# A two-layer S5, Hyena and pooling step: another opening, another order of tiles, and layer 0's output projection by halves of the tokens

## The chip, the cores and the metric

The kernel runs on one core of a Trainium2 chip. The metric is the device time of one execution in microseconds; the kernel before takes 1530.49 us (median of three runs, 1528.8 to 1534.48). The engines of the core run side by side, each through its own instructions in a fixed order: TensorE (PE, with its weight loads as PEld), VectorE (DVE), ScalarE (ACT), GpSimd (POOL) and SyncE (SP), which here issues nearly all DMAs.

## The reference

One step of a hybrid diffusion backbone of two layers. 640 tokens of 1024 numbers (512 latent ones and 128 of context) go through

```
for l in range(2):
    shift, scale, gate = split(silu(cond) @ w_mod[l] + b_mod[l])      # one row for latents, one for context
    h   = rms_norm(x, norm_g[l]) * (1 + scale) + shift
    u_a, g_a, u_b, g_b, u_c, g_c, m = split(h @ w_in[l])              # 1024 -> 7168
    y_a = s5_branch(u_a, state, ...) * silu(g_a)                      # two-way scan, 32 groups of 64 complex states
    y_b = hyena_branch(u_b, ...) * silu(g_b)                          # short conv, then long convs by FFT, order 2
    y_c = pool_branch(u_c, ...) * silu(g_c)                           # centred means over 2, 4, 8, 16 less the token
    merged = sum of sigmoid(m_i) * (y_i @ w_br_i[l])
    x = x + gate * (merged @ w_out[l])
```

and a last RMSNorm. The Hyena filters come from a small sine network over positions, `h = sin(freq*(sin(freq*(z @ w1 + b1)) @ w2 + b2)) @ w3`, times a decaying window, plus a bias; each `fft_long_conv` uses one of them. All arithmetic is float32.

## The kernel before

**Products.** Activations lie with channels on the partitions and tokens along the free side, in two halves of 320 tokens (`HT`). A float32 product is made of three matmuls: `split` (L235) rounds a tile to a high part (`wh`, a cast on ACT, L238) and takes the rest (`wl`, a subtract on DVE, L239), and `linear` (L245) adds `wh*hi`, `wh*lo` and `wl*hi` (L261 to L263). It goes through a weight tile in chunks of 128 x 512: one load `wr` of 256 KB, one cast, one subtract, and for each half of the tokens 4 x 3 matmuls of 320 columns. An input tile has two chunks. The buffers `wr`, `wh`, `wl` are three deep, and so are the PSUM tiles `mm` and those of the tag `b`.

**Opening** (`run`). The loads of the inputs, `mlp` (the filter network up to `fh`), `s5_disc` (the S5 constants), the squares of X (`square`, L577: a square on ACT and a sum over the channel tiles on DVE, L589), the chunks of the modulation (`mod_chunk`, L404), `rinv` (L610: the sum of squares by matmuls of one column, L599, then an inverse root of 13 small steps on a given engine, a diagonal `rdg` on DVE, a matmul that broadcasts it, `rbc` L635, and a copy to `rr`), `make_h` (L645) and four `filter` calls (L488: `fw`, `fwp` from `fh`, a window and bias on DVE, `fold`, and a transform `fps` L549 to L551).

**A layer** (`layer`, L1400). `u_a` (L668) makes the four input tiles of the scan, copies them to `ua`, and writes them to DRAM (`ud`), from where they come back in another layout (`ug`). Then eight S5 blocks run: `s5_gen` builds the matrices of a block (DVE and GpSimd L873 to L875, matmuls `khp`, a copy `kh`, a write `kd` to DRAM and the loads `mt` from it) and `s5_run` scans (`pz` L944, four scans on DVE, `yp` L974). Behind each block stand two or three input tiles of other branches, from the list `beside`: 12 of `conv_u` (L986: evictions to a buffer `raw`, of which there are two, a scaling on ACT and two steps on DVE, L1003 and L1005), then 4 of `gate_b` (L1030) and 4 of `ahead` (L1008), which have an eviction on ACT and little else. After the blocks come the GLU, the Hyena convolutions, the merges, and `out_proj` (L1250) with eight tiles.

**The boundary.** Between the layers the eight output tiles of layer 0, each over both halves, are followed by `rinv` on GpSimd and `make_h` for both halves; the filters of layer 1 stand between them. Layer 1's own output projection, at the end, goes through the eight tiles once for each half.

**What sets the order.** The program is written in the order above, and a scheduler at build time moves instructions against each other on each engine by estimated costs, within their dependences; on the chip every engine keeps the order that it was given. Tile pools fix how many tiles of one name may be alive.

Of the kernel before, what the change touches and what calls it, by code (L numbers as in the profile page):

```python
# [43 lines left out]
L642 = 642  # L44
PAD = 8
# [6 lines left out]
C_ID, C_ONE, C_MT, C_CM, C_DM, C_SEL, C_POSR, C_POSC, C_EL, C_ER, C_PI2, C_EPS, C_MAG, C_N = range(14)  # L52


def _cst_layout():
    sizes = [P, P, NA + NBW, CZ, H, 2, 4 * 8, 4 * 64, 15, 11, 1, 1, 1]
    offs = np.concatenate([[0], np.cumsum(sizes)])
    return [int(v) for v in offs]
# [18 lines left out]
def constants():  # L77
# [38 lines left out]
    cst[:, CO[C_MAG]] = MAGIC  # L116

# [105 lines left out]
class Body:  # L223
# [264 lines left out]
    def filter(self, l, o, hf, F, buf=None):  # L488
# [33 lines left out]
        v.tensor_tensor(out=hx[0:1, 2], in0=hx[0:1, 2], in1=br[0:1], op=ALU.add)  # L522
        v.tensor_tensor(out=hq[64:65], in0=hq[64:65], in1=br[64:65], op=ALU.add)
# [67 lines left out]

    def rsum(self, halves, tag):
# [17 lines left out]
    def rinv(self, halves, e, tag="b", root=False):  # L610
# [3 lines left out]
        ps = self.rsum(halves, tag)  # L614
# [14 lines left out]
        prs = []  # L629
        for i in range(len(halves)):  # L630
            dg = self.N.tile([P, nh, 64], F32, tag="ht", name="rdg", bufs=2)[0:64]
# [4 lines left out]
            rr = self.N.tile([P, HT], F32, tag="rr", name="rr", bufs=2)  # L636
            nc.scalar.copy(rr, pr)
            prs.append((rr, pr))
        return prs
# [5 lines left out]
    def make_h(self, l, X, half, rr):  # L645
        nc = self.nc
        sm, sg = self.smod[l]
        t0 = half * HT
        for kk in range(KD):
            t = self.N.tile([P, HT], F32, tag="ht", name="ht", bufs=2)  # L650
            for s, e, _, ci in self.segs(half):
                b = sm[:, kk, ci:ci + 1]
                hi = self.hhi[:, kk, t0 + s:t0 + e]
                lo = self.hlo[:, kk, t0 + s:t0 + e]
                if kk in (3, 6):
                    nc.gpsimd.tensor_tensor(out=t[:, s:e], in0=X[:, kk, t0 + s:t0 + e], in1=rr[:, s:e], op=ALU.mult)
                    nc.scalar.activation(t[:, s:e], t[:, s:e], AF.Identity, scale=sg[:, kk, ci:ci + 1], bias=b)
                    nc.scalar.copy(hi, t[:, s:e])
                    nc.vector.tensor_tensor(out=lo, in0=t[:, s:e], in1=hi.bitcast(F32), op=ALU.subtract)  # L659
                    continue  # L660
                nc.vector.scalar_tensor_tensor(out=t[:, s:e], in0=X[:, kk, t0 + s:t0 + e],
# [846 lines left out]
```

## Time and profile before

| | |
|---|---|
| profiled execution, us | 1534.17 |
| its span, us | 1532.4 |
| granted TensorE clock, mean over the span | 0.976 |
| median of three runs, us | 1530.49 |
| ACT, POOL busy | 44%, 34% of the span |
| cast `wh`, 128 x 512, on ACT | 0.619 us, 316 times |
| load `wr` from w_out, 256 KB, issue to landing | 3.0 us, 48 times |

The span runs from the first to the last instruction of the profiled execution; the time also holds the little that lies around it. Busy shares are averages over stages with different limits, so the stages are looked at one by one: a window of the trace gives the busy time of each engine and the clock that PE was granted there, and a list of waits tells what an engine stood idle for.

### The profile page before, as it was taken

The numbers are of one execution on the slowest core, as the hardware profiler recorded it, in microseconds if no ns is written. First come the engines' busy times: TensorE is split into PE (matmuls) and PEld (weight loads), VectorE is DVE, ScalarE is ACT, GpSimd is POOL, SyncE is SP. The second block draws the span as 40 slices with busy tenths as digits, with TensorE's granted clock in tenths as the row PEclk, the third lists the DMA queues.
The fourth block names the chain that finished last, engine by engine and source line by source line (L and its number), as shares of the span: only waits on it lengthen the run. The fifth ranks groups of instructions, "written<-read, shape, count | busy, mean of one in ns | idle before, by whom it ended". The sixth has DMA issues, their size and how long they took to land.

```text
span 1532.4 us, 28365 instructions
## 1 busy us (share of the span) xinstructions
PE 1435.3 (94%) x10812; PEld 1372.2 (90%) x10812; DVE 1125.5 (73%) x1951; ACT 672.0 (44%) x1454; POOL 524.9 (34%) x473
## 2 busy tenths in 40 slices
PE   3998899999999999999998897989999999999997
PEld 1688888999999998999997787989999999999996
DVE  8996998854777795555678879896557778866665
ACT  3574545434333342344345644544443334344443
POOL 0033433500343334553323733443003444166401
PEclk9899999999999999999998899999999999999998
DMA  9535122244322246444752342223622223322154
GB/s 313 188 112 132 57 72 70 71 146 123 99 71 77 76 134 234 157 151 139 230 159 81 110 113 68 71 71 94 172 89 81 83 70 106 115 83 83 35 178 153
DMA packets 120464, 178.74 MB, mean 117 GB/s; under 512 B 33944, under 2 KB 58152, under 8 KB 119817
## 3 DMA queue, kind: packets, MB, share of 16 engines
q1 hardware_dynamic: 115737, 170.58, 36.5%
q0 software_dynamic: 1152, 5.77, 1.1%
q8 instruction: 85, 1.39, 0.4%
q10 hardware_dynamic: 3440, 0.59, 0.2%
q14 instruction: 50, 0.41, 0.1%
HBM read 152.71 MB, written 24.18 MB: 115 GB/s over the span
## 4 chain that ended last, share of the span: by engine, by line
PE 68%; DVE 15%; DMA 6%; issue 5%; ACT 3%; SPq 2%; POOL 1%; POOLq 0%; ACTq 0%; DVEq 0%
PE mm L261 15%; PE mm L263 15%; PE mm L262 15%; PE mm L333 3%; PE mm L335 3%; PE mm L334 3%; DVE wl L239 2%; PE inva L1145 1%; SPq L914 1%; DVE i L874 1%; PE invb L1145 1%; PE yp L976 1%; PE modp L404 1%; DVE vx L1003 1%; DVE hlo L665 1%
## 5 line engine op out<-in xcount | busy, mean ns | idle before, releaser
L261 PE MATMUL mm<-hhi,wh 128*128 128x320 f32 x1408 | 446.1, 318 | 15.3 <-ACT raw L996 9.0
L263 PE MATMUL mm<-hhi,wl 128*128 128x320 f32 x1408 | 440.4, 314 | 8.5 <-DVE wl L239 6.3
L262 PE MATMUL mm<-hlo,wh 128*128 128x320 f32 x1408 | 442.4, 314 | 0.5 <-DVE hlo L659 0.4
L239 DVE TENSOR_TENSOR wl<-wr,wh 128x512 fp32r<-128x512 f32 x316 | 265.9, 843 | 114.4 <-ACT wh L238 111.5
L238 ACT CAST wh<-wr 128x512 fp32r<-128x512 f32 x316 | 195.5, 619 | 269.1 <-PE mm L262 188.9
L261 PEld LDWEIGHTS mm<-hhi,wh 128*128 128x128 f32 x1408 | 269.9, 192 | 20.8 <-ACT raw L996 10.0
L263 PEld LDWEIGHTS mm<-hhi,wl 128*128 128x128 f32 x1408 | 269.5, 192 | 9.5 <-DVE wl L239 6.8
L262 PEld LDWEIGHTS mm<-hlo,wh 128*128 128x128 f32 x1408 | 270.1, 192 | 1.7 <-DVE hlo L659 1.2
L262 PE MATMUL mm<-mlo,wh 128*128 128x320 f32 x256 | 79.6, 312 | 0.5 <-DVE mlo L242 0.4
L261 PE MATMUL mm<-mhi,wh 128*128 128x320 f32 x256 | 79.1, 312 | 0.5 <-ACT wh L238 0.4
L263 PE MATMUL mm<-mhi,wl 128*128 128x320 f32 x256 | 78.8, 309 | 0.4 <-DVE wl L239 0.4
L873 POOL TENSOR_TENSOR ow<-cw,po 128x512 f32<-128x512 f32 x32 | 41.9, 1328 | 96.6 <-PE yp L976 96.5
L875 POOL TENSOR_TENSOR i<-i,i 128x1024 f32<-128x1024 f32 x16 | 40.5, 2529 | 100.6 <-DVE i L873 71.8
L1244 DVE SCALAR_TENSOR_TENSOR mth<-mth,mm 128x320 f32<-128x320 f32 x64 | 31.1, 486 | 52.5 <-PE mm L263 52.5
L1246 POOL TENSOR_TENSOR macc<-macc,mth 128x320 f32<-128x320 f32 x32 | 35.0, 1099 | 86.4 <-DVE mth L1244 86.4
L239 DVE TENSOR_TENSOR wl<-ws,wh 128x512 fp32r<-128x512 f32 x48 | 42.7, 889 | 29.7 <-ACT wh L238 28.6
L333 PE MATMUL mm<-hhi,wh 128*128 128x320 f32 x192 | 59.9, 312 | 0.0
L335 PE MATMUL mm<-hhi,wl 128*128 128x320 f32 x192 | 59.4, 309 | 0.0
L334 PE MATMUL mm<-hlo,wh 128*128 128x320 f32 x192 | 59.4, 309 | 0.0
L238 ACT CAST wh<-ws 128x512 fp32r<-128x512 f32 x48 | 29.8, 621 | 60.2 <-PE mm L334 32.3
L1052 POOL TENSOR_TENSOR ps<-pu 128x663 f32<-128x663 f32 x8 | 12.3, 1540 | 120.4 <-ACT pu L1045 120.4
L1246 POOL TENSOR_TENSOR acc<-acc,mth 128x320 f32<-128x320 f32 x32 | 37.7, 1179 | 44.4 <-DVE mth L1244 44.3
(421 smaller groups left out, 3809.9 us busy)
## 6 DMA issues: line engine op xcount, KB each, us to landing
wr<-w_in SPq DMA_DIRECT2D x224, 256.0 KB, 2.6
wm<-w_mod SPq DMA_DIRECT2D x48, 512.0 KB, 5.4
wr<-w_out SPq DMA_DIRECT2D x48, 256.0 KB, 3.0
hd<-hs SPq DMA_DIRECT2D x32, 256.0 KB, 2.3
hsr<-hd SPq DMA_DIRECT2D x32, 256.0 KB, 2.6
mt<-kd SPq DMA_DIRECT2D x128, 32.0 KB, 1.8
wr<-w_br_a SPq DMA_DIRECT2D x16, 256.0 KB, 2.6
wr<-w_br_b SPq DMA_DIRECT2D x16, 256.0 KB, 2.7
```

Of the source, the lines that this page charges most:

```text
L238: nc.scalar.copy(hi, src)
L239: nc.vector.tensor_tensor(out=lo, in0=src, in1=hi.bitcast(F32), op=ALU.subtract)
L261: nc.tensor.matmul(ps[i], wh[:, ks], at(hi, k, sl), start=(k == 0), stop=False)
L262: nc.tensor.matmul(ps[i], wh[:, ks], at(lo, k, sl), start=False, stop=False)
L263: nc.tensor.matmul(ps[i], wl[:, ks], at(hi, k, sl), start=False, stop=(k == kt - 1))
L333: nc.tensor.matmul(out, wh[:, ks], xh, start=(k == 0), stop=False)
L334: nc.tensor.matmul(out, wh[:, ks], xl, start=False, stop=False)
L335: nc.tensor.matmul(out, wl[:, ks], xh, start=False, stop=(k == 3))
L873: eng.tensor_tensor(out=out[:, r], in0=hb(r), in1=pb(0), op=ALU.mult)
L875: e.tensor_tensor(out=out, in0=out, in1=tmp, op=ALU.add)
L1244: v.scalar_tensor_tensor(out=o[:, sl], in0=th[:, sl], scalar=1.0, in1=ps, op0=ALU.add, op1=ALU.mult)
L1246: nc.gpsimd.tensor_tensor(out=acc[:, sl], in0=acc[:, sl], in1=th[:, sl], op=ALU.add)
```

## The change

Five things are done in another way. (1) In the opening the squares are summed by PE alone, in matmuls of one column (`square_pe`), the inverse root is taken right behind them, and `make_h` goes over the tokens once, in two segments. (2) The bias of a Hyena filter, added by DVE in two operations on one partition, is added by two matmuls with one row of weights. (3) `u_a` has four buffers, two of them under the tag `raw`, and in layer 1 goes through the tiles once for each half of the tokens. (4) The list `beside` is mixed: three convolution tiles and two lighter ones to every pair of blocks, the last four channel tiles first. (5) Layer 0's output projection goes through the eight tiles once for each half, with `rinv` on DVE and `make_h` of a half behind each pass. Some memsets move from DVE to GpSimd.

```diff
@@ filter
                 nc.tensor.matmul(fp if t == 4 else fw[:, t], fh[:, t * P:t * P + P], w, start=(i == 0),
-                                 stop=(i == len(ws) - 1))
+                                 stop=(i == len(ws) - 1 and t not in (2, 4)))
+            if t in (2, 4):
+                r = slice(0, 1) if t == 2 else slice(64, 65)
+                nc.tensor.matmul(fp if t == 4 else fw[:, t], self.k(C_BR)[r], br[r], start=False, stop=True)
...
-        v.tensor_tensor(out=hx[0:1, 2], in0=hx[0:1, 2], in1=br[0:1], op=ALU.add)
-        v.tensor_tensor(out=hq[64:65], in0=hq[64:65], in1=br[64:65], op=ALU.add)
@@
+    def square_pe(self, X, kk, half, ps):
+        nc = self.nc
+        nh = HT // 64
+        sq = self.N.tile([P, HT], F32, tag="sq", name="sq", bufs=2)
+        nc.scalar.activation(sq, X[:, kk, half * HT:half * HT + HT], AF.Square)
+        for j in range(nh):
+            c = half * nh + j
+            nc.tensor.matmul(ps[:, c:c + 1], sq[:, j * 64:j * 64 + 64], self.k(C_ONE)[:, 0:1],
+                             start=(half == 0 and kk == 0 and j == 0),
+                             stop=(half == 1 and kk == KD - 1 and j == nh - 1))
@@ make_h
-    def make_h(self, l, X, half, rr):
+    def make_h(self, l, X, segs, rr):
...
-            t = self.N.tile([P, HT], F32, tag="ht", name="ht", bufs=2)
-            for s, e, _, ci in self.segs(half):
+            t = self.N.tile([P, segs[-1][1] - base], F32, tag="ht", name="ht", bufs=2)
+            for s, e, ci in segs:
...
@@ u_a
+        ua = [SP.tile([P, NT, CW], F32, name=f"ua{i}") if i < 2 else
+              SP.tile([P, NT, CW], F32, tag="raw", name="ua", bufs=2) for i in range(4)]
         for i in range(4):
-            ua = uas[i % 2]
-            nc.vector.memset(ua[:, :, 64:65], 0.0)
...
+            nc.gpsimd.memset(ua[i][:, :, 64:65], 0.0)
+        for halves in ((0,), (1,)) if l else ((0, 1),):
+            for i in range(4):
...
+                self.linear(self.I['w_in'][l, i].rearrange("p k n -> p (k n)"), KD, self.hhi, self.hlo, cb, halves)
+                if halves[-1] == 1:
+                    nc.sync.dma_start(self.ud[l].rearrange("t q c -> q t c")[i * P:i * P + P], ua[i])
@@ run, opening
+                    ssq = self.PS.tile([P, 512], F32, tag="mm", name="ssq", bufs=3)[0:64, 0:2 * (HT // 64)]
                     for kk in range(KD):
-                        self.square(X, kk, 0)
+                        self.square_pe(X, kk, 0, ssq)
...
+                    rr = self.rinv((0, 1), nc.vector, "mm", ps=ssq)
                     self.mod_turn(0, 2, self.mod_chunk(0, 2, M, "mm"), "mm")
...
-                    rr = [r for r, _ in self.rinv((0, 1), nc.vector, "mm")]
...
-                for half in range(2):
-                    self.make_h(0, X, half, rr[half])
+                self.make_h(0, X, ((0, LS, 0), (LS, T, 1)), rr)
@@ run, boundary
                             for n in range(8):
-                                self.out_proj(l, X, n, mhi, mlo, last, (0, 1))
+                                self.out_proj(l, X, n, mhi, mlo, last, (0,))
...
-                            rr = [r for r, _ in self.rinv((0, 1), nc.gpsimd, "mm")]
-                            for half in range(2):
-                                self.make_h(l + 1, X, half, rr[half])
-                            for hf in range(2):
-                                self.filter(l + 1, 1, hf, F, fb() if hf else None)
+                            rr = self.rinv((0,), nc.vector, "mm")
+                            self.make_h(l + 1, X, ((0, HT, 0),), rr)
+                            for n in range(8):
+                                self.out_proj(l, X, n, mhi, mlo, last, (1,))
+                                if n == 3:
+                                    self.filter(l + 1, 1, 0, F)
+                            rr = self.rinv((1,), nc.vector, "mm")
+                            self.make_h(l + 1, X, ((HT, LS, 0), (LS, T, 1)), rr)
+                            self.filter(l + 1, 1, 1, F, fb())
@@ layer
-            beside = [lambda i=i: self.conv_u(l, i, vx[i // 4][:, i % 4, :], SP) for i in range(12)]
-            beside += [lambda i=i: self.gate_b(l, i, S, vx[2]) for i in range(4)]
-            beside += [lambda i=i: self.ahead(l, 40 + i, AF.Tanh, 0.5, SP) for i in range(4)]
+            heavy = [lambda i=i: self.conv_u(l, i, vx[i // 4][:, i % 4, :], SP) for i in (*range(8, 12), *range(8))]
+            gates = [lambda i=i: self.gate_b(l, i, S, vx[2]) for i in range(4)]
+            ahead = [lambda i=i: self.ahead(l, 40 + i, AF.Tanh, 0.5, SP) for i in range(4)]
+            light = ahead[:2] + gates + ahead[2:]
+            beside = []
+            for i in range(4):
+                h, g = heavy[3 * i:3 * i + 3], light[2 * i:2 * i + 2]
+                beside += [h[0], g[0], h[1], h[2], g[1]]
```

PE in the opening, from the end of the filter network to the first filter: before, two stretches of modulation (`modp`) stand there; the names are those of the text above.

```order
L461 MATMUL mlpp<-mlp,w_111 128x320 x2
L404 MATMUL modp<-wm,cs 32x512 x8
L415 MATMUL modt<-cst,mp 128x2 x4
L404 MATMUL modp<-wm,cs 32x512 x4
L511 MATMUL fw_663<-w_349,fh_87 128x256 x4
L511 MATMUL fwp<-w_349,fh_87 128x256
```

The same place now:

```order
L464 MATMUL mlpp<-mlp,w_111 128x320 x2
L603 MATMUL ssq<-cst,sq 64x1 x45
L514 MATMUL fw_664<-w_406,fh_87 128x256 x3
L518 MATMUL fw_664<-br,cst 128x256
L514 MATMUL fw_664<-w_406,fh_87 128x256
L514 MATMUL fwp<-w_406,fh_87 128x256
L518 MATMUL fwp<-br,cst 128x256
```

The sums of squares have come to this place, the modulation has left it for later, and each filter has two matmuls more.

ScalarE in the first S5 blocks of layer 0: before, one convolution tile (`raw`) follows another.

```order
L996 COPY raw<-mm 128x320
L238 CAST wh<-wr 128x512
L996 COPY raw<-mm 128x192
L996 COPY raw<-mm 128x128
L1001 ACTIVATE vx_1051<-raw,par_143 128x642
L238 CAST wh<-wr 128x512
L996 COPY raw<-mm 128x320
```

The same place now, where `gst` is the result of an `ahead` tile:

```order
L1017 COPY raw<-mm 128x192
L1017 COPY raw<-mm 128x128
L1022 ACTIVATE vx_1054<-raw,par_143 128x642
L241 CAST wh<-wr 128x512
L1034 ACTIVATE gst<-mm 128x320
L241 CAST wh<-wr 128x512
L1034 ACTIVATE gst<-mm 128x320
```

A lighter tile stands behind the first convolution tile.

PE at the end of the boundary: before, the broadcasts `rbc` of both halves stand among the transforms of layer 1's filters.

```order
L550 MATMUL fps<-flo,fr 128x256
L551 MATMUL fps<-fhi,fr 128x256
L635 MATMUL rbc<-rdg,cst 128x320 x2
L550 MATMUL fps<-flo,fr 128x256
L551 MATMUL fps<-fhi,fr 128x256
```

The same place now, behind the tiles of the second half:

```order
L614 MATMUL ssq<-cst,acc 64x1 x5
L554 MATMUL fps<-flo,fr 128x256
L555 MATMUL fps<-fhi,fr 128x256
L614 MATMUL ssq<-cst,sq 64x1 x5
L652 MATMUL rbc<-rdg,cst 128x320
L264 MATMUL mm<-hhi,wh 128x320
L265 MATMUL mm<-hlo,wh 128x320
L266 MATMUL mm<-hhi,wl 128x320
```

The broadcast of the second half stands between the last sums of squares and the first matmuls of the scan input of the first half, with nothing else there.

## Rows read from the trace of the kernel before

**Rows 1.** Page, part 1: engine, busy us, share of the span, instructions.
```profile
PE 1435.3 (94%) x10812; PEld 1372.2 (90%) x10812; DVE 1125.5 (73%) x1951; ACT 672.0 (44%) x1454; POOL 524.9 (34%) x473
```

**Rows 2.** Windows, layer 0 blocks: stretch, length, busy PE, PEld, DVE, ACT, POOL; granted clock, DMA.
```profile
145.00:195.00 50.00, 46.16 (x460) 44.35 (x461) 46.92 (x63) 24.61 (x65) 20.09 (x11) 0.97 0.22 67
195.00:244.00 49.00, 45.15 (x408) 43.51 (x408) 43.01 (x71) 27.52 (x70) 16.41 (x12) 0.93 0.28 75
244.00:295.00 51.00, 45.36 (x388) 44.49 (x385) 43.86 (x54) 23.59 (x62) 23.22 (x16) 0.93 0.24 71
295.00:341.00 46.00, 46.00 (x455) 45.26 (x454) 30.76 (x38) 15.51 (x38) 10.94 (x11) 1.00 0.38 111
```

**Rows 3.** The same for the blocks of layer 1.
```profile
895.00:945.00 50.00, 43.93 (x456) 42.07 (x454) 47.60 (x66) 24.81 (x66) 21.59 (x12) 1.00 0.21 61
945.00:994.00 49.00, 44.65 (x406) 43.64 (x408) 41.42 (x67) 27.51 (x70) 16.00 (x11) 0.93 0.27 76
994.00:1044.00 50.00, 44.53 (x393) 43.66 (x388) 43.57 (x55) 23.38 (x62) 23.59 (x16) 0.97 0.24 72
1044.00:1089.00 45.00, 45.00 (x448) 44.27 (x447) 30.15 (x38) 15.40 (x37) 10.25 (x11) 1.00 0.39 111
```

**Rows 4.** Windows of DVE line L1003, one a convolution tile: stretch, length, busy, count.
```profile
244.00:295.00 51.00, 4.45 (x3) 0.93 0.24 71
295.00:341.00 46.00, 0.00 (x0) 1.00 0.38 111
```

**Rows 5.** PE's waits in 145 to 345: waiting line, releaser, us in total, times, longest.
```profile
PE yp L974 <- DMA mt<-kd: 8.0, 4, 3.6
PE mm L261 <- ACT raw L996: 5.1, 2, 3.1
```

**Rows 6.** PE's waits in 895 to 1095.
```profile
PE yp L974 <- DMA mt<-kd: 11.5, 5, 3.7
PE mm L261 <- ACT raw L996: 3.9, 2, 2.6
```

**Rows 7.** Windows, the boundary between the layers, and the last output projection.
```profile
800.00:845.00 45.00, 38.31 (x246) 33.71 (x247) 37.09 (x78) 26.54 (x59) 13.30 (x21) 0.89 0.27 94
845.00:880.00 35.00, 27.36 (x157) 26.58 (x157) 29.45 (x35) 22.02 (x53) 27.71 (x19) 0.85 0.38 104
738.70:880.00 141.30, 126.98 (x832) 121.24 (x832) 107.25 (x187) 72.05 (x157) 56.51 (x60) 0.93 0.47 144
1487.00:1515.50 28.50, 28.39 (x197) 26.95 (x196) 19.29 (x43) 14.30 (x28) 2.55 (x3) 1.00 0.65 206
```

**Rows 8.** PE's longest wait in 738 to 895.
```profile
PE mm L263 <- DVE wl L239: 5.0, 1, 5.0
```

**Rows 9.** Windows, the opening: both parts up to the first DRAM round trip.
```profile
0.00:36.50 36.50, 10.39 (x32) 4.00 (x32) 30.00 (x111) 13.20 (x28) 1.47 (x6) 0.95 0.94 310
36.50:130.00 93.50, 86.16 (x588) 70.29 (x589) 84.04 (x178) 55.94 (x127) 24.86 (x20) 0.93 0.46 145
```

**Rows 10.** One of PE's waits in 0 to 130.
```profile
PE mm L263 <- DVE ua L672: 2.3, 1, 2.3
```

**Rows 11.** PE timeline 0 to 60: start, us of the run, engine, line, tiles, count.
```profile
26.02 4.45 PE L404 MATMUL modp<-wm,cs 128*32 128x512 f32 x16
...
39.61 1.99 PE L511 MATMUL fw<-w,fh 64*128 64x256 f32 x8
...
58.31 0.74 PE L599 MATMUL ssq<-cst,acc 128*64 128x1 f32 x10
```

**Rows 12.** DVE line L589: ns min/median/max, first and last start, shapes.
```profile
L589 DVE TENSOR_TENSOR acc<-acc,sq x12: 480/483/485, 19.5 to 40.3; 128x320 f32<-128x320 f32 x12
```

**Rows 13.** DVE lines by shape in 845 to 880: count, busy us, mean ns, idle.
```profile
L239 DVE TENSOR_TENSOR wl<-wr,wh 128x512 fp32r<-128x512 f32 x7 | 10.4, 1492 | 5.5 <-ACT wh L238 5.5
```

**Rows 14.** The same in 1458.5 to 1515.5.
```profile
L239 DVE TENSOR_TENSOR wl<-wr,wh 128x512 fp32r<-128x512 f32 x29 | 19.8, 689 | 9.7 <-ACT wh L238 9.7
```

**Rows 15.** POOL timeline, first step of the inverse root at the boundary.
```profile
809.23 0.20 POOL L626 TENSOR_SCALAR ry<-rx 64x10 int32<-64x10 int32 x1 [12.51 <-ACT rx L625]
```

More of the change, by code (lines that the diff above doesn't have):

```diff
@@ L44 @@
 L642 = 642
+RAW = NT * CW
 PAD = 8
@@ L116, in constants @@
     cst[:, CO[C_MAG]] = MAGIC
+    for r in (0, 64):
+        cst[r, CO[C_BR] + r] = 1.0 / (1.0 + f32(0.05))
     fmax = 15
@@ L608, in newton, with rinv @@
         e.tensor_tensor(out=y, in0=y, in1=t, op=ALU.mult)
-    def rinv(self, halves, e, tag="b", root=False):
+    def rinv(self, halves, e, tag="b", root=False, ps=None):
         nc = self.nc
@@ L613, in rinv @@
         n = nh * len(halves)
-        ps = self.rsum(halves, tag)
+        if ps is None:
+            ps = self.rsum(halves, tag)
         x = self.N.tile([64, n], F32, tag="rx", name="rx", bufs=2)
@@ L652, in make_h @@
                 b = sm[:, kk, ci:ci + 1]
-                hi = self.hhi[:, kk, t0 + s:t0 + e]
-                lo = self.hlo[:, kk, t0 + s:t0 + e]
+                hi = self.hhi[:, kk, s:e]
+                lo = self.hlo[:, kk, s:e]
+                tv, rv = t[:, s - base:e - base], rr[:, s - base:e - base]
                 if kk in (3, 6):
[L656 to L659, printed above, removed]
+                    nc.gpsimd.tensor_tensor(out=tv, in0=X[:, kk, s:e], in1=rv, op=ALU.mult)
+                    nc.scalar.activation(tv, tv, AF.Identity, scale=sg[:, kk, ci:ci + 1], bias=b)
+                    nc.scalar.copy(hi, tv)
+                    nc.vector.tensor_tensor(out=lo, in0=tv, in1=hi.bitcast(F32), op=ALU.subtract)
@@ L660, in make_h @@
                     continue
-                nc.vector.scalar_tensor_tensor(out=t[:, s:e], in0=X[:, kk, t0 + s:t0 + e],
-                                               scalar=sg[:, kk, ci:ci + 1], in1=rr[:, s:e], op0=ALU.mult,
-                                               op1=ALU.mult)
-                nc.scalar.activation(hi, t[:, s:e], AF.Identity, bias=b)
-                nc.vector.scalar_tensor_tensor(out=lo, in0=t[:, s:e], scalar=b,
-                                               in1=hi.bitcast(F32), op0=ALU.add, op1=ALU.subtract)
@@ L668, in u_a @@
-    def u_a(self, l, S, uas):
+                nc.vector.scalar_tensor_tensor(out=tv, in0=X[:, kk, s:e], scalar=sg[:, kk, ci:ci + 1], in1=rv,
+                                               op0=ALU.mult, op1=ALU.mult)
+                nc.scalar.activation(hi, tv, AF.Identity, bias=b)
+                nc.vector.scalar_tensor_tensor(out=lo, in0=tv, scalar=b, in1=hi.bitcast(F32),
+                                               op0=ALU.add, op1=ALU.subtract)
+    def u_a(self, l, SP):
         nc = self.nc
+        ua = [SP.tile([P, NT, CW], F32, name=f"ua{i}") if i < 2 else
+              SP.tile([P, NT, CW], F32, tag="raw", name="ua", bufs=2) for i in range(4)]
@@ L987, in conv_u @@
         nc = self.nc
-        raw = U.tile([P, L642 + 2], F32, tag="raw", name="raw", bufs=2)
+        raw = U.tile([P, RAW], F32, tag="raw", name="raw", bufs=2)
         nc.vector.memset(raw[:, 0:1], 0.0)
@@ L1009, in ahead @@
         nc = self.nc
-        st = U.tile([P, L642 + 2], F32, tag="raw", name="gst", bufs=2)[:, 0:T]
+        st = U.tile([P, RAW], F32, tag="raw", name="gst", bufs=2)[:, 0:T]
         def cb(half, ps):
```

36 lines of the change are left out of this document (17 added, 19 removed).

## The prediction, made before the changed kernel had run

> **What bounds the kernel now.** I read the busy shares first. TensorE (PE) is busy for 94% of the span and VectorE (DVE) for 73% [rows 1], so time can only come from PE's idle stretches, from stretches in which PE was granted less than its full clock, and from PE instructions that go away. The second view is a table of windows cut at the kernel's stages, read by two columns: PE's busy time against the window's length, and the granted clock. In each layer's eight S5 blocks the first three pairs of blocks leave PE 3.8 to 6.1 us short, mostly at 0.93 to 0.97 of its clock, while the last pair has no idle time and the full clock [rows 2, 3]. The same rows show what differs: DVE is busy for 85 to 95% of the first three windows and for 67% of the last. The 12 convolution tiles (evicted by ScalarE into a buffer called raw, then one ScalarE and two long DVE steps each) all end in the first three windows, three of them in the third and none in the last [rows 4], which has light tiles alone. Third, the waits of PE in these stretches: 8.0 and 11.5 us for the loads of mt (a block's kernel matrix, which goes out to DRAM and comes back), 5.1 and 3.9 us for the two raw buffers [rows 5, 6].
>
> The boundary between the layers (second half of the output projection, inverse root, make_h, the next layer's scan input u_a) takes 141.3 us, of which PE is busy 126.98 at 0.93 of the clock; the idle 14.3 us lie after 800 us, about half in front of the scan input (800 to 845) and half within it (845 to 880) [rows 7]. The longest single wait there is 5.0 us for a DVE subtract [rows 8]. In the opening PE does 10.39 us of work in the first 36.5 us and is nearly full, 86.16 of 93.5 us at 0.93, from there to the first DRAM round trip [rows 9].
>
> Everything is summed against the profiled execution, 1534.2 us (span 1532.4 and 1.8 around it); it lies 3.7 us above the median of 1530.5.
>
> **The opening.** Removed from DVE: 12 additions of 0.483 us, 5.8 us [rows 12], of which ten start before 36.5 us, where DVE is the engine that the filter network goes through (30.0 us busy) [rows 9]. Some small S5 steps are pulled ahead in their place, so I let the first filter matmul come 3 us sooner than 39.61 [rows 11]. The squares' sums become 80 matmuls of one column instead of 20; ten took 0.74 us, so 80 cost 5.9 us, all in PE's idle 26 us at the front [rows 9, 11]. But the modulation leaves that place: 24 of its matmuls stood ahead of the first filter, at 4.45/16 = 0.28 us each 6.7 us, and now come behind it [rows 11]. Behind the first filter PE therefore gets +6.7, -1.5 (20 old sum matmuls), and +2.0 for the bias: eight matmuls with one row of weights, which no row shows; the nearest, 64 rows deep, is 1.99/8 = 0.25 us [rows 11] (ends 0.1 and 0.4 us each). That makes +7.2 us against 7.3 us of idle there [rows 9]. The wait for a reused ua buffer, 2.3 us, goes with four buffers [rows 10]. The eight one-row bias additions that leave DVE I count at nothing, since PE is the fuller engine there, and the memsets that go to GpSimd as well, which is busy for 1.47 of the first 36.5 us [rows 9]. Of the idle I let half be filled: 7.2 - 3 - 3.7 = 0.5. I take 0; ends -5 (all the idle filled, the early start kept, half of the 6 us that 7% of the clock is worth) and +8 (nothing hides).
>
> **The S5 blocks.** The new order gives three convolution tiles and two light tiles to every pair of blocks. DVE's load is then the mean of the four windows, 164.6/196 = 84% in layer 0 and 162.7/194 = 84% in layer 1 [rows 2, 3]. What can be won at most is the idle time, 13.3 and 15.9 us, and the clock, 7.7 and 4.5 us (busy time by one minus the clock, window by window): 41 us, and that is one end. The other end has a row too: the third window already has three convolution tiles and light ones beside them [rows 4], a load of 86 or 87%, and it stalls as the others do, 51 us against 46 and 50 against 45 for the last [rows 2, 3]. If every pair became like the third, layer 0 would take 4 x 51 = 204 instead of 196 and layer 1 200 instead of 194: +14. But the third pair inherits what the second left on DVE, and it has no part in the waits for raw, which come where convolution tiles follow each other. So the value that I take is nearer to that row than to the last: the 9.0 us of waits for raw go [rows 5, 6], since two convolution tiles now follow each other directly only once in a pair of blocks, and 2 us of clock with them; the 19.5 us of waits for mt stay, since their chain (an eviction by ScalarE, one DVE step, a DRAM write and read) has the same PE work beside it as before and DVE is no emptier than in the third window. -11; ends +14 and -41.
>
> **The boundary.** Done half by half, the first half's inverse root and make_h lie under eight half tiles of PE work, and the second half's make_h under the scan input of the first half. The pattern itself has a row: the last output projection, half by half already, keeps PE busy 28.39 of 28.5 us [rows 7]. So the 6.7 us of idle in 800 to 845 go, and with them the clock lost there, 11% of 38.3 = 4.2 us. Of the 7.6 us of idle and 4.1 us of clock in 845 to 880 most stays: it comes from GpSimd and DVE preparing the S5 matrices together, which is not moved; I let 3 us go. Against it stand the bias matmuls, +2.0, and one new wait: the broadcast of the second half's inverse root stands in PE's queue directly ahead of the scan input, which does not need it but is queued behind it. From the last sums to it are a ScalarE step, 13 small steps (0.20 us each on GpSimd [rows 15], now on DVE: 2.6 us) and the diagonal. With what lies between the steps I take 4.5 us; if other DVE work stands between, 8.
>
> Each half needs its own weights: 16 more chunk loads, casts and subtracts in the projection and 8 in the scan input. The loads are 24 x 256 KB beside a DMA share of 0.47, and the casts go to ScalarE, which is busy for 72 of the 141 us [rows 7]; both are hidden. The subtract took 0.69 us where GpSimd was nearly idle [rows 7, 14] and 1.49 where GpSimd was busy for 27.7 of 35 us [rows 7, 13]. So 16 x 0.69 + 8 x 1.49 = 23 us on DVE, which has 107.25 of 141.3 us there: 130 us, below the 95% that DVE reaches in its fullest window [rows 3]. I hide them. Sum: +2.0 + 4.5 - 6.7 - 4.2 - 3 = -7.4, taken as -7; ends +7 (nothing recovered) and -17 (all idle and all lost clock recovered).
>
> Stretches with waits are the ones below the full clock here: 0.89 and 0.85 against 1.00 [rows 7]. The Trainium skill (TensorE: Matmul & The Clock Gate, "Why this matters for your kernels") asks for no idle gaps between bursts of matmuls. By it the new 4.5 us wait would be followed by a stretch at the lower clock; if that cost as much as the 4.2 us lost in 800 to 845, the boundary would be -3 and the time 1519.
>
> **The sum.** 0 - 11 - 7 = -18: 1534.2 - 18 = 1516; from the median it would be 1512.5. I say 1515.
>
> **The rivals.**
> 1. Every pair of blocks becomes like the third. The mechanism: DVE is at 84 to 87% everywhere, the one DVE step in the chain to mt stands behind convolution steps in all eight blocks, and the last pair loses its light load. For it: the third window [rows 2 to 4]. Against it: the mean over the layer holds two windows that are fuller. The blocks give +14, the rest -7: 1541. The break-even of the whole change is at blocks +7, that is 0.9 a pair, pairs of 49.9 us in layer 0 and 49.4 in layer 1; it is slower by more than noise from pairs of 50.8 and 50.3.
> 2. Much more is won. For it: the last pair at 67% has no idle at all, so the stalls may end at a load between 67 and 85%, and the clock comes back with the waits. Blocks -28, boundary -10, opening -3: 1493. Against it: the third window, and 7 us more PE work behind the first filter.
> 3. The change does not do what it says at the boundary: the broadcast ahead of the scan input keeps the old wait in a new place, 8 us and the clock behind it, so the boundary gives +4 instead of -7, with the blocks' -11: 1527. For it: nothing stands between the two on PE; against it: the step is one of 320 tokens, behind short work.
> 4. DVE becomes the bound at the boundary: the second half's make_h, the S5 preparation and the chunk subtracts in one queue, with three chunk buffers between DVE and PE; one such wait is there already, 5.0 us [rows 8]. At a mean of 2.1 us for a subtract, 24 are 50 us; (107.25 + 50)/0.95 = 166 us instead of 141, +25; with the blocks' -11 the time is 1548. Break-even with -11 is where DVE has 152 x 0.95 = 145 us, a mean subtract of 1.6 us. Against it: the 16 in the projection meet little GpSimd work, and a mean of 0.96 is what I expect.
>
> **Chances and range.** The forecast, within 1504 to 1526, has 0.45; rival 1 (1530 to 1550) 0.10; rival 2 (1483 to 1504) 0.24; rival 3 (1518 to 1533) 0.14; rival 4 (1533 to 1560) 0.07. A change of 0.5%, 7.7 us, is about what a measurement of this kernel can tell from none; within it is 1522.8 to 1538.1. Faster: most of the forecast (0.40), all of rival 2 and a third of rival 3 (0.05): 0.69. Slower: 0.06 of rival 1 and 0.04 of rival 4: 0.10. The rest, 0.21, is no change. The forecast's own range is 1504 to 1526; 1492 to 1536 leaves out two fifths of rival 2, half of rival 1 and most of rival 4, 0.20 together.
>
> **What would show it.** Right: the four pairs of blocks look like each other, 48 to 49 us each, with no wait for raw over 1 us and PE's waits for mt still 15 to 22 us in both layers together; the output projection of layer 0 in two stretches of about 30 us with PE full; one wait of 4 to 5 us of PE on the broadcast, then the scan input; the subtract's mean below 1.5 us there; the first filter matmul at about 36 us and the end of the first scan input within 4 us of 130. Wrong: pairs of 51 us (rival 1) or of 46 (rival 2); a wait on the broadcast above 7 us (rival 3); several waits of PE for wl at the boundary (rival 4); the first scan input later than 134 us, for which the sum has no room.

## The result, and the profile after

The changed kernel takes 1549.44 us (median of four runs, 1547.79 to 1552.48) against 1531.53 us of the kernel before: ratio 1.0117, 95% interval 1.0089 to 1.0144. It is slower by 1.2%, and the time lies 13 us above the wider of the prediction's ranges (1492 to 1536).

PE is as busy as before by share, and does more in a longer span (part 1 of the page, to [rows 1]):

```profile
PE 1463.0 (94%) x10964; PEld 1392.9 (90%) x10964; DVE 1117.6 (72%) x1943; ACT 684.7 (44%) x1469; POOL 525.3 (34%) x474
```

From the traces, the moments at which the stages begin or end, in us from the span's start (first or last instruction on the tile named):

| | before | after | difference |
|---|---|---|---|
| first scan matmul `pz`, layer 0 | 145.0 | 152.0 | +7.0 |
| first step of the GLU (`ghi`), layer 0 | 349.2 | 356.7 | +7.5 |
| first matmul of the output projection | 734.7 | 739.7 | +5.0 |
| last `X` of layer 0 | 801.5 | 838.2 | +36.7 |
| end of make_h for layer 1 | 844.2 | 858.5 | +14.3 |
| first `pz`, layer 1 | 894.8 | 912.7 | +17.9 |
| first `ghi`, layer 1 | 1098.5 | 1114.7 | +16.2 |
| last `X` of layer 1 | 1520.1 | 1536.9 | +16.8 |

So there are two losses: 7 us in the opening and 13 us at the boundary (173.0 us from the first projection matmul to the first scan matmul, 160.1 before). The blocks with the mixed order of tiles changed by +0.5 and -1.7 us, the stretches behind them by -2.5 and +0.6, far from the -11 forecast. These moments are of one execution each: layer 0's blocks take 206.0 and 200.9 us in two traces of one kernel (mixed_only and mixed_again, below), so a difference of a few us in one stage says little by itself.

**The opening.** Windows up to the end of the first scan input (columns as in the windows above), against [rows 9]:

```profile
0.00:36.50 36.50, 21.70 (x162) 18.96 (x163) 28.10 (x108) 14.18 (x31) 3.12 (x14) 1.00 0.88 289
36.50:54.00 17.50, 17.50 (x52) 11.77 (x51) 15.71 (x45) 10.20 (x23) 0.00 (x0) 1.00 0.36 88
54.00:137.00 83.00, 77.55 (x481) 60.48 (x481) 60.14 (x87) 42.44 (x92) 26.37 (x19) 0.98 0.48 154
```

The clock column reads 1.00 in the second row, and PE is busy all the time. The timeline of PE shows what this hides (start, us, operation, tiles, count):

```profile
16.49 7.63 PE L603 MATMUL ssq<-cst,sq 128*64 128x1 f32 x70 [3.76 <-ACT sq L600]
...
26.47 6.56 PE L603 MATMUL ssq<-cst,sq 128*64 128x1 f32 x60
...
37.25 2.92 PE L514 MATMUL fw<-w,fh 64*128 64x256 f32 x6
40.10 1.22 PE L518 MATMUL fw<-br,cst 1*128 1x256 f32 x2
...
53.89 1.92 PE L514 MATMUL fw<-w,fh 64*128 64x256 f32 x6
55.74 0.69 PE L518 MATMUL fw<-br,cst 1*128 1x256 f32 x2
...
62.63 1.92 PE L407 MATMUL modp<-wm,cs 128*32 128x512 f32 x16
64.48 1.56 PE L514 MATMUL fw<-w,fh 64*128 64x256 f32 x6
```

Six records of the same filter matmul take 2.92 us at 37.25 and 1.56 us at 64.48: until 53.9 us PE ran at half speed, the lower of its two levels. The 160 records of one-column matmuls ahead of it ran at that level too (60 records in 6.56 us, 1.1 us for ten, where ten took 0.74 us [rows 11]) and did not lift it. In the kernel before, the modulation stood there. It began at the lower level as well (16 records in 4.45 us [rows 11], 1.92 us later in that trace), and the first filter behind it ran at full speed at once, 8 records in 1.99 us [rows 11]. 16.6 us at half speed are 8 us of work. The kernel before has such a stretch too, but a shorter one: from 60.2 to 66.6 us, behind 30 records of one-column matmuls, and there the granted clock reads 0.50 (60 to 66 us). The rows also show that an fp32 matmul leaves two records: 80 one-column matmuls are 160 records and took 7.6 + 6.6 + 3.5 = 17.7 us, and a bias matmul is two, 1.2 us at half and 0.69 at full speed.

From 36.5 us to the first scan matmul, before and after:

```profile
36.50:145.00 108.50, 97.84 (x668) 81.71 (x668) 91.36 (x191) 61.98 (x140) 28.28 (x22) 0.94 0.50 148
36.50:152.00 115.50, 110.05 (x674) 87.03 (x673) 83.05 (x149) 59.04 (x128) 28.77 (x20) 0.99 0.51 147
```

PE stands idle for 5.4 us instead of 10.7, so half of the idle time was filled, as forecast. But its work grew by 12.2 us, where 7.2 were forecast. By lines of the kernel: the bias matmuls 7.1 us, the filter matmuls 5.6 more (at half speed), the modulation 2.3 more, the sums of squares 2.5 less.

**The boundary.** The whole stretch, before and then after, and three stretches of after:

```profile
734.70:894.80 160.10, 144.14 (x991) 137.91 (x990) 119.92 (x208) 79.56 (x173) 62.54 (x63) 0.94 0.49 147
```

```profile
739.70:912.70 173.00, 150.01 (x1014) 140.48 (x1013) 138.19 (x240) 94.61 (x200) 62.26 (x58) 0.93 0.58 175
845.00:860.00 15.00, 13.84 (x77) 13.28 (x77) 13.03 (x34) 11.97 (x30) 4.22 (x12) 0.83 0.27 86
860.00:880.00 20.00, 15.78 (x96) 13.76 (x94) 15.25 (x13) 14.03 (x31) 14.57 (x12) 1.00 0.57 170
880.00:898.00 18.00, 8.45 (x43) 8.45 (x44) 18.00 (x17) 8.18 (x23) 13.87 (x8) 0.72 0.41 92
```

DVE has 18 us more to do (138.2 against 119.9). The subtracts alone are 21.8 us more, near the 23 that the prediction had for them (before, then after):

```profile
L239 DVE TENSOR_TENSOR wl<-wr,wh 128x512 fp32r<-128x512 f32 x28 | 25.7, 922 | 12.2 <-ACT wh L238 12.1
L242 DVE TENSOR_TENSOR wl<-wr,wh 128x512 fp32r<-128x512 f32 x53 | 47.5, 902 | 15.9 <-ACT wh L241 15.6
```

Over the stretch DVE is 80% busy. But from 880 to 898 us it is busy for 18.00 of 18 us and PE for 8.45. PE's waits in 743 to 900, to [rows 8]:

```profile
PE mm L266 <- DVE wl L242: 13.8, 6, 9.6
PE mm L264 <- ACT wh L241: 3.5, 2, 3.2
PE rbc L652 <- DVE rdg L649: 3.5, 1, 3.5
```

The wait on the broadcast is 3.5 us, 4.5 forecast. The waits for `wl` are 13.8 us, where the kernel before had 5.0 in one wait [rows 8]; 9.6 us of them are one wait. DVE's timeline ahead of its end at 889.55 us:

```profile
877.80 1.54 DVE L894 TENSOR_TENSOR i<-bb,pi 128x512 f32<-128x512 f32 x1
879.26 1.54 DVE L895 TENSOR_TENSOR i<-bb,pi 128x512 f32<-128x512 f32 x1
880.73 1.54 DVE L894 TENSOR_TENSOR i<-bb,pi 128x512 f32<-128x512 f32 x1
882.19 1.53 DVE L895 TENSOR_TENSOR i<-bb,pi 128x512 f32<-128x512 f32 x1
883.65 3.10 DVE L940 TENSOR_TENSOR tt<-ph 128x352 f32<-128x352 f32 x2
886.67 5.75 DVE L242 TENSOR_TENSOR wl<-wr,wh 128x512 fp32r<-128x512 f32 x3
```

The subtracts of three chunks start at 886.67, behind six steps of the S5 preparation (`i`, `tt`) that take 1.5 us each, and take 1.9 us each themselves (0.69 where GpSimd is nearly idle [rows 14]). The scan input's second half, which PE has in its queue, stands still for that long.

This order is not new. In mixed_only, a run below that has the boundary of before, the same steps stand ahead of a subtract that PE stands still for, 5.6 us; the list of waits puts it down to DVE's memset of `raw`, which ends right behind that subtract (872.90 us; a row of its waits and one of DVE's timeline):

```profile
PE mm L266 <- DVE raw L1011: 5.6, 1, 5.6
870.06 2.84 DVE L242 TENSOR_TENSOR wl<-wr,wh 128x512 fp32r<-128x512 f32 x1
```

So what the halves changed is the length of the wait, 9.6 us instead of 5.0 to 5.6. By halves a chunk has 12 matmuls behind it and not 24, with three chunk buffers as before, so PE can run out of chunks sooner while DVE is at the preparation. That fits, but no run tests it by itself.

**The S5 blocks.** Windows of layer 0 after, to [rows 2], and PE's waits in the blocks of layer 0, then of layer 1, to [rows 5, 6]:

```profile
152.00:203.00 51.00, 47.10 (x472) 45.81 (x472) 45.12 (x64) 24.18 (x64) 21.38 (x12) 0.97 0.30 89
203.00:252.00 49.00, 47.14 (x439) 45.93 (x438) 36.91 (x57) 26.35 (x66) 19.97 (x14) 0.93 0.24 70
252.00:302.00 50.00, 45.03 (x428) 43.46 (x428) 43.60 (x59) 25.06 (x64) 22.08 (x16) 1.00 0.24 71
302.00:352.00 50.00, 48.20 (x417) 47.58 (x412) 32.00 (x50) 17.38 (x42) 5.50 (x7) 0.97 0.38 109
```

```profile
PE yp L995 <- DMA mt<-kd: 5.5, 3, 2.4
PE yp L997 <- DVE w L989: 4.2, 3, 1.6
PE mm L264 <- ACT raw L1017: 1.8, 2, 1.1
```

```profile
PE mm L264 <- ACT raw L1017: 7.5, 2, 6.6
PE yp L997 <- DVE w L989: 3.7, 5, 1.1
PE yp L995 <- DMA mt<-kd: 3.2, 2, 2.1
```

The stalls are spread, not gone: no window is free of idle time any more, waits for `mt` fell from 19.5 to 8.7 us, waits for `w` (the scan's result on DVE) grew from 0.7 to 7.9 us, and `raw` is at 9.3 us, 9.0 before. DVE's load did not become even: it is 88, 75, 87 and 64% of the four windows, though two or three convolution tiles end in each. In the last window their first step takes 0.88 us on DVE and GpSimd is busy for 5.5 us; in the second it takes 1.57 us and GpSimd is busy for 20.0. So the last pair of blocks was not light on DVE through its light tiles alone.

### The profile page after: what moved, and what is told of

It is laid out like the page before. It is cut to its first block, busy times and chain, and to the rows that moved or that the text cites. A ratio compares the mean times of both kernels' runs of the same rounds, so it can differ in the third digit from the quotient of the medians.

```text
span 1549.7 us, 28772 instructions
## 1 busy us (share of the span) xinstructions
PE 1463.0 (94%) x10964; PEld 1392.9 (90%) x10964; DVE 1117.6 (72%) x1943; ACT 684.7 (44%) x1469; POOL 525.3 (34%) x474
## 4 chain that ended last, share of the span: by engine, by line
PE 70%; DVE 13%; DMA 6%; issue 5%; ACT 3%; POOL 2%; SPq 2%; POOLq 0%; DVEq 0%; ACTq 0%
PE mm L264 14%; PE mm L266 14%; PE mm L265 14%; PE mm L336 3%; PE mm L338 3%; PE mm L337 3%; DVE wl L242 2%; PE modp L407 2%; PE inva L1166 1%; PE yp L997 1%; PE invb L1166 1%; PE fw L514 1%; DVE kk L983 1%; DVE i L895 1%; DVE kk L982 1%
## 5 line engine op out<-in xcount | busy, mean ns | idle before, releaser
L242 DVE TENSOR_TENSOR wl<-wr,wh 128x512 fp32r<-128x512 f32 x340 | 286.9, 845 | 108.8 <-ACT wh L241 105.5
L241 ACT CAST wh<-wr 128x512 fp32r<-128x512 f32 x340 | 210.1, 618 | 277.3 <-PE mm L265 200.3
L896 POOL TENSOR_TENSOR i<-i,i 128x1024 f32<-128x1024 f32 x16 | 44.1, 2758 | 88.6 <-DVE i L894 67.3
L338 PE MATMUL mm<-hhi,wl 128*128 128x320 f32 x192 | 59.4, 309 | 0.0
L337 PE MATMUL mm<-hlo,wh 128*128 128x320 f32 x192 | 59.4, 309 | 0.0
L241 ACT CAST wh<-ws 128x512 fp32r<-128x512 f32 x48 | 29.8, 621 | 60.2 <-PE mm L337 32.3
L264 PEld LDWEIGHTS mm<-mhi,wh 128*128 128x128 f32 x256 | 49.7, 195 | 7.2 <-ACT wh L241 5.6
```

Source lines behind the costliest of these rows:

```text
L241: nc.scalar.copy(hi, src)
L242: nc.vector.tensor_tensor(out=lo, in0=src, in1=hi.bitcast(F32), op=ALU.subtract)
L264: nc.tensor.matmul(ps[i], wh[:, ks], at(hi, k, sl), start=(k == 0), stop=False)
L337: nc.tensor.matmul(out, wh[:, ks], xl, start=False, stop=False)
L338: nc.tensor.matmul(out, wl[:, ks], xh, start=False, stop=(k == 3))
L896: e.tensor_tensor(out=out, in0=out, in1=tmp, op=ALU.add)
```

## The experiments

The times are medians; the ratios are to runs of the kernel before on the same chip. First the parts of the change one by one.

**dve_bias.**

```diff
-                nc.tensor.matmul(fp if t == 4 else fw[:, t], self.k(C_BR)[r], br[r], start=False, stop=True)
...
+        v.tensor_tensor(out=hx[0:1, 2], in0=hx[0:1, 2], in1=br[0:1], op=ALU.add)
+        v.tensor_tensor(out=hq[64:65], in0=hq[64:65], in1=br[64:65], op=ALU.add)
```

> The changed kernel with the Hyena bias added by DVE again (16 matmuls with one row of weights out). Theory: PE is the bound in both places where filters stand, so they cost their full time: 8 x 0.63 us at the boundary, about 6.6 us in the opening (three of them at 1.15 us): 1549 - 11 = 1538, within 1534 to 1543. Rival, the bias matmuls lie beside other work: 1547 to 1551.

1551.63 us, ratio 1.0126 (1.0106 to 1.0145): nothing won. My theory on the bias matmuls fell. Without them PE stands idle for 13.5 us from 36.5 us to the first scan matmul instead of 5.4, partly for the first filter's results (rows of PE, with the wait in brackets):

```profile
48.77 0.58 PE L552 MATMUL fps<-fhp,frp 128*128 128x256 f32 x1 [2.78 <-ACT fhp L241]
50.94 0.58 PE L552 MATMUL fps<-fhi,fr 128*128 128x256 f32 x1 [1.58 <-ACT fhi L241]
```

and the filter's records stay at half speed until 59.4 us instead of 53.9. The first scan matmul comes at 153.6 us, against 152.0.

**mod_front.**

```diff
-                    rr = self.rinv((0, 1), nc.vector, "mm", ps=ssq)
                     self.mod_turn(0, 2, self.mod_chunk(0, 2, M, "mm"), "mm")
...
                     self.mod_turn(0, 0, self.mod_chunk(0, 0, M, "mm"), "mm")
+                    rr = self.rinv((0, 1), nc.vector, "mm", ps=ssq)
```

> The changed kernel with the inverse root of the opening called behind the third modulation chunk, as before; the squares are still summed by 80 matmuls of one column, but the modulation stands among them and among the first filters again. Theory: the first filters run at half speed from 37 to 54 us because PE had only one-column matmuls to do before; with the 512-column matmuls of the modulation there they run at full speed, 4 to 8 us are won: 1541 to 1545. Rival, the one-column matmuls in front are themselves the loss (18 us of PE): 1548 to 1551.

1562.76 us, ratio 1.0198 (1.0173 to 1.0222): the opposite of what I expected, the first scan matmul at 162.2 us. The first filter did run at full speed, and the next one no longer; the window shows the clock that was granted from 54 to 97 us:

```profile
47.15 1.56 PE L514 MATMUL fw<-w,fh 64*128 64x256 f32 x6
...
59.15 2.93 PE L514 MATMUL fw<-w,fh 64*128 64x256 f32 x6
```

```profile
54.00:97.00 43.00, 43.00 (x157) 28.50 (x154) 26.04 (x55) 14.73 (x30) 3.87 (x4) 0.60 0.22 74
```

PE was busy all the time and at 0.60 of the clock for 43 us, 17 us of work lost. So the modulation in front did not secure the speed. It fell at about 50.5 us, right behind 20 records of one-column matmuls; the fall at 60.2 us in the kernel before has 30 of them ahead of it.

**old_opening** (with the inverse root as in mod_front and the bias as in dve_bias).

```diff
-                        self.square_pe(X, kk, 0, ssq)
+                        self.square(X, kk, 0)
...
-                self.make_h(0, X, ((0, LS, 0), (LS, T, 1)), rr)
+                self.make_h(0, X, ((0, HT, 0),), rr)
+                self.make_h(0, X, ((HT, LS, 0), (LS, T, 1)), rr[:, HT:])
```

> The changed kernel with the opening of before (squares summed on DVE, inverse root late, make_h by halves) and the bias on DVE everywhere; boundary by halves and mixed tiles kept. Theory: the opening's 7 us and the 5 us of bias matmuls at the boundary go: 1549 - 12 = 1537, 1534 to 1540, first scan matmul at about 145. Rival, the loss is all in the boundary's DVE work: 1545 or more.

1542.67 us, ratio 1.0065 (1.0044 to 1.0086): the first scan matmul is at 145.4 us, so the opening's 7 us are back. They are not the clock alone: from 36.5 us to the first scan matmul PE was granted 0.89 of it here, less than before (0.94), and had stretches at half speed too (0.50 from 48 to 54 us).

```profile
36.50:145.40 108.90, 99.95 (x668) 84.36 (x668) 86.64 (x192) 63.12 (x140) 27.43 (x22) 0.89 0.51 152
```

The boundary is as long as in the changed kernel (172.9 us), so the bias matmuls cost nothing there.

**old_boundary.**

```diff
-        for halves in ((0,), (1,)) if l else ((0, 1),):
+        for halves in ((0, 1),):
...
-                                self.out_proj(l, X, n, mhi, mlo, last, (0,))
+                                self.out_proj(l, X, n, mhi, mlo, last, (0, 1))
...
+                            rr = self.rinv((0, 1), nc.gpsimd, "mm")
```

> The changed kernel with the boundary of before (out_proj over both halves, inverse root on GpSimd, make_h for both halves behind it, u_a of layer 1 over both halves at once); opening, bias matmuls and mixed tiles as changed. Theory: the boundary from the first output-projection matmul to the first scan matmul, 173 us in the changed kernel and 160 before, goes back to 160 plus 5 for the bias matmuls: 1549 - 8 = 1541, 1538 to 1545. Rival, the halves hide make_h as meant and the loss is elsewhere: 1549 or more.

1536.19 us, ratio 1.0031 (1.0016 to 1.0046): 13 us back; the boundary takes 161.7 us.

**mixed_only** and, in more rounds, **mixed_again** (old_opening and old_boundary together: the mixed order, four `ua` buffers and memsets on GpSimd remain).

> The kernel before with the mixed order of input tiles alone (and the four ua buffers and the memsets on GpSimd; opening, bias on DVE and boundary as before). Theory: the stages of the changed kernel put the mixed order at -0.5 and +0.5 us in the two layers' S5 blocks and -2.4 us in each layer's stretch behind them: 1526, 1523 to 1530. Rival 1 of the prediction (every pair like the third): 1540 or more.

> The mixed order alone once more, in more rounds: is it faster than the kernel before? From the first time: ratio 0.9986, between 0.997 and 1.000.

1528.25 us, ratio 0.9986 (0.9974 to 0.9999), and 1528.66, ratio 0.9975 (0.9959 to 0.9991). It is faster than the kernel before by 0.1 to 0.3%; rival 1 of the prediction is out.

Then the boundary.

**filters_behind.**

```diff
+                            wd = F.tile([P, 256], F32, tag="w3", name="w3", bufs=1)
+                            nc.scalar.copy(wd[:, 0:1], X[:, KD - 1, T - 1:T])
                             rr = self.rinv((1,), nc.vector, "mm")
```

> The changed kernel with the last two filters of layer 1 held back by a dependence until the last X of the second half is there (one copy of 128 numbers), so that the second half pass is projection alone and the filters' matmuls stand behind the broadcast, among the scan input. Theory now: the boundary is a chain, last X, inverse root, make_h, S5 preparation (which waits for the space of X) and scan input; in the changed kernel all filters were done before the last X, which came 31.7 us later after the start of the projection than before (98.5 against 66.8), and left PE nothing to do beside the chain. The last X comes about 15 us sooner, the first scan matmul of layer 1 10 to 15 us sooner: 1535 to 1540. Rival, DVE's subtracts behind the S5 preparation are the loss: DVE has the same work, 1547 to 1552.

1550.49 us, ratio 1.013 (1.0114 to 1.0147): that theory fell. The last X did come 13 us sooner, at 825.2, but make_h ended at 860.6 (858.5 in the changed kernel): DVE now had the filters' windows and folds in between and was full,

```profile
845.00:860.00 15.00, 15.00 (x111) 14.50 (x109) 14.73 (x32) 11.09 (x27) 4.13 (x6) 1.00 0.36 121
```

as the third busy time of the window, DVE's, shows (14.73 of 15 us).

**whole_ua.**

```diff
-        for halves in ((0,), (1,)) if l else ((0, 1),):
+        for halves in ((0, 1),):
```

> The changed kernel with the scan input of layer 1 done over both halves at once (8 chunk loads, casts and subtracts fewer), the output projection by halves kept. Theory (chain from the last X): the chain is the same and the scan input must now wait for the second half's make_h, but needs half of the subtracts: within 4 us of the changed kernel, 1546 to 1554. Rival, the 8 added subtracts of 1.1 us beside the S5 preparation are the loss: 1538 to 1542.

1541.64 us, ratio 1.0064 (1.0043 to 1.0085): 8 us back, as the rival had it. From the end of make_h to the first scan matmul there are 48.7 us, 54.2 in the changed kernel. What is left to old_boundary, 5 us, is the projection by halves beside a whole scan input.

**ua_halves** (against old_boundary).

```diff
-        for halves in ((0, 1),):
+        for halves in ((0,), (1,)) if l else ((0, 1),):
```

> The run old_boundary (1536: output projection over both halves, inverse root on GpSimd) with the scan input of layer 1 by halves again. Theory: the halved scan input costs 5 to 7 us wherever the projection stands: 1541 to 1544. Rival, the halves let the scan input start under the second half's make_h and the loss came from the projection by halves: 1530 to 1536.

1550.16 us, ratio 1.0123 (1.0091 to 1.0154): 14 us more than old_boundary, again with one wait of 9.6 us for `wl`. It is also as slow as the changed kernel, which has the projection by halves as well: the two costs do not add, and beside a halved scan input the halved projection costs nothing that these times show. In the two traces the difference is 10 us: 6.7 us lie before the first scan matmul, about 4 in the S5 blocks behind it; why those are longer I can't say.

**split_twice.**

```diff
             self.split(wh, wl, wr)
+            if twice:
+                self.split(wh, wl, wr)
```

> The mixed order alone (run mixed_only, 1528), with the cast and the subtract of each of the 8 weight chunks of layer 1's scan input done twice into the same buffer; loads and matmuls are unchanged. That is the DVE and ScalarE work that the halved scan input adds, and nothing else of it. Theory now: beside the S5 preparation DVE and GpSimd are the bound, so the 8 subtracts lengthen the stretch from the end of make_h to the first scan matmul of layer 1 from 49.4 to 54 or 55 us, as in every run with the halved scan input: 1533 to 1536. Rival, it is the order of the halves (the second half's chunks behind the first, more loads), not the split work: 1526 to 1530.

1537.94 us, ratio 1.0037 (1.0024 to 1.0051), against 0.9986 for mixed_only beside the same kernel: 8 to 10 us for 8 casts and 8 subtracts, with neither loads nor matmuls more. The boundary grew from 159.3 to 166.6 us. PE waits for `wl` 9.5 us in all, 5.6 in mixed_only (above), but the longest wait is as long as there, 5.5 us, and not 9.6:

```profile
PE mm L268 <- DVE wl L242: 9.5, 2, 5.5
```

So the added DVE and ScalarE work costs time there, in other waits than the halves do. A chunk's second cast also has to follow its first subtract here, which reads what that cast writes, a chain that the halves do not have; the run does not tell the two apart.

**quiet.**

```diff
-        kr(e, ow, o1, self.cw, self.po, 1)
+        if l == 1 and b < 2:
+            e.memset(ow, 0.0)
+        else:
+            kr(e, ow, o1, self.cw, self.po, 1)
```

> The changed kernel with GpSimd's share of the S5 preparation left out in the first two blocks of layer 1 (the output matrices ow are set to zero there in place of seven GpSimd steps each, so layer 1's scan output of these blocks is not computed). DVE's order from make_h to the first scan matmul is the same: six S5 steps stand ahead of the subtract that PE waited 9.6 us for. Theory, each is slow because GpSimd works beside it: from 880 us on they take 0.7 instead of 1.5 us, the wait falls to 5 us or less, the first scan matmul of layer 1 comes 4 to 9 us sooner, 1540 to 1545. Rival, the order alone is the loss: the wait stays at 8 us or more, 1546 to 1550.

1544.37 us, ratio 1.008 (1.0057 to 1.0103), 5 us less. From the end of make_h to the first scan matmul of layer 1 there are 49.8 us, 54.2 in the changed kernel; another 4.8 us in this trace were won ahead of the output projection, where the edit changes nothing. DVE's order is the same, its steps are not (to compare with the timeline above):

```profile
877.25 0.68 DVE L895 TENSOR_TENSOR i<-bb,pi 128x512 f32<-128x512 f32 x1
877.86 0.68 DVE L894 TENSOR_TENSOR i<-bb,pi 128x512 f32<-128x512 f32 x1
878.46 0.68 DVE L895 TENSOR_TENSOR i<-bb,pi 128x512 f32<-128x512 f32 x1
879.06 3.12 DVE L943 TENSOR_TENSOR tt<-ph 128x352 f32<-128x352 f32 x2
882.10 1.88 DVE L242 TENSOR_TENSOR wl<-wr,wh 128x512 fp32r<-128x512 f32 x3
```

```profile
PE mm L266 <- DVE wl L242: 8.5, 7, 4.9
```

Three of the four `i` steps take 0.68 us instead of 1.54 and the subtracts 0.63 instead of 1.9, and the longest wait for `wl` is 4.9 instead of 9.6 us. So about half of that wait is this work of GpSimd beside DVE. What remains is the order, the subtracts behind the preparation, with what GpSimd still does there. The kernel before has that order, and a wait of 5.0 us, with all of GpSimd's work.

Last, the opening once more. **old_squares** (the inverse root stays early).

```diff
-                        self.square_pe(X, kk, 0, ssq)
+                        self.square(X, kk, 0)
...
-                self.make_h(0, X, ((0, LS, 0), (LS, T, 1)), rr)
+                self.make_h(0, X, ((0, HT, 0),), rr)
+                self.make_h(0, X, ((HT, LS, 0), (LS, T, 1)), rr[:, HT:])
```

> The changed kernel with the squares of the opening summed on DVE again (12 additions, 20 one-column matmuls instead of 80) and make_h by halves; the inverse root is called early as changed, so the modulation stays behind the first filters. Theory: the opening's 7 us come from the modulation and the bias matmuls behind the first filters, while PE has run at half speed until then; the 60 further one-column matmuls lie in idle time and cost nothing: first scan matmul at 150 to 154, 1547 to 1551. Rival, the one-column matmuls are the loss: first scan matmul at 145 to 148, 1541 to 1545.

1562.28 us, ratio 1.0224 (1.0173 to 1.0276), the first scan matmul at 159.6 us: neither expectation. With the modulation gone to later and no one-column matmuls in its place, PE is idle for 9 us ahead of the first filter and at half speed until 56 us. It falls to half speed again at 59.3 us (granted 0.77 from 60 to 66), with filter and bias matmuls ahead of it and no one-column ones, so the falls in these traces have no one cause that I can name. Taking either half of the new opening back makes it worse; taking both back helps. Which part of it the 7 us are, no run shows.

## Why the prediction was wrong

- **The opening, "I take 0"**: it was +7, and the terms that failed are the work behind the first filter, +7.2 forecast and +12.2 measured, and "all in PE's idle 26 us at the front" with no price for the speed behind it. The sum read the timeline's counts as matmuls; they are records, two for each of these matmuls, and those of the modulation in front were at half speed. So the 80 sums cost 17.7 us and not 5.9; the eight bias matmuls 7.1 us and not 2.0 (an end of the range had 3.2); the modulation 2.3 more and not 6.7. The filter matmuls, which had no term at all, cost 5.6 us more, since the first 16.6 us behind the one-column matmuls ran at half speed. Half of the idle time was filled, as forecast, and the first filter came 2.4 us sooner, 3 forecast. Why the whole is 7 us later stays open: without the bias matmuls PE waits instead (dve_bias), a full-speed first filter did not help (mod_front), and old_opening won the 7 us back with a mean clock of 0.89. Shown is only that it is the new opening, of which neither half can go back alone.
- **The S5 blocks, -11**: -1 by the table, -3 us in the whole time with all that mixed_again wins. The step that failed is the load: "DVE's load is then the mean of the four windows" came out as 88, 75, 87 and 64% in layer 0. The 9 us of waits for `raw` did not go; those for `mt`, which I had let stand, fell by 11 us, and new ones for the scan's DVE steps took 7 us in their place. The bound that I had from the third window (+14) was too pessimistic.
- **The boundary, -7**: +13. The new wait on the broadcast was sized about right (3.5 for 4.5 us), and so was DVE's added work (21.8 for 23 us). The step that failed is "I hide them", of the chunk preparation that halving doubles: 8 chunks more in the scan input cost 8 us beside the halved projection (whole_ua) and 14 without it (ua_halves), the projection's halves 5 us or nothing. I compared DVE's load with the length of the whole stretch, 130 of 141 us; but PE waits for particular subtracts, which stand behind the S5 preparation, where DVE is busy for 18.00 of 18 us from 880 us on, and the wait that was 5.0 us became 9.6. GpSimd's work beside DVE is about half of that (quiet); the rest is argued from the order, not tested.
- **Rival 4** named the place, the queue and a time of 1548, and had a chance of 0.07. Its time came near by luck, +25 at the boundary with -11 in the blocks, where +13, -1 and the opening's +7 were measured. Its price was wrong as well: it asked for a mean subtract above 1.6 us, and the mean was 0.90 over the boundary and 1.09 from 843 us on. Not the mean tells but which instructions stand ahead of a subtract that PE is waiting for.
- **The lower clock behind a wait** was at the boundary as the second reckoning had it: the windows behind the wait on the broadcast and around the 9.6 us wait were granted 0.83 and 0.72. The Trainium skill (TensorE: Matmul & The Clock Gate, "Why this matters for your kernels") asks for no idle gaps between bursts of matmuls. Here the trace agrees: 0.50 was granted from 845 to 850 us, right behind the first of these waits, and 1.00 from 850 to 860.

## What to carry to other kernels

Cost work that is added to an engine in the stretch where it lands, against what is already queued there, not against the stage's mean load: DVE at 76% over 141 us did not hide 8 more subtracts in the 40 us in which GpSimd works beside it. Halving a product over its tokens doubles the weights' preparation and leaves each prepared chunk half of the matmuls; here it cost up to 14 us. Before pricing matmuls from a timeline, check whether its counts are matmuls or records, and at which of PE's two levels they ran.

## What was not expected of the hardware

The granted clock of a window can read 1.00 while PE runs at half speed: 6 records in 2.92 us at 37.25 and in 1.56 us at 64.48 us, both under 1.00. In these traces that is so in the first tens of us of the span; later stretches at half speed read 0.50 (60 to 66 us in the kernel before). 160 records of one-column matmuls, 17.7 us with hardly a gap, did not bring PE to the higher level, and the 16.6 us of filter matmuls behind them ran at the lower one too. DVE steps of 128 x 512 took 1.54 us beside GpSimd and 0.68 when GpSimd's steps were left out, with nothing else changed on DVE.
